# A two-layer transformer on one core: inputs laid out by features, first modulation in quarters

## The chip, the core and the metric

The program runs on one core of a Trainium2 chip. The metric is device time in microseconds (us) of one execution. The engines are PE (TensorE, matrix products), PEld (its weight loads), DVE (VectorE), ACT (ScalarE), POOL (GpSimd) and SP (SyncE, which issues most DMA transfers here). Each engine works its own list of instructions in order, and waits at an instruction for what it needs from other engines.

## The reference, cut to what matters

```python
for l in range(2):                              # DEPTH = 2, D = 1024
    sh1, sc1, gt1, sh2, sc2, gt2 = adaln(c, w_ada[l], b_ada[l])      # silu(c) @ w_ada + b_ada
    csh1, csc1, cgt1, ... = adaln(c_ctx, w_ada[l], b_ada[l])
    h  = rms_norm(x,   g_mix[l]) * (1 + sc1)  + sh1                  # x: 512 x 1024
    hc = rms_norm(ctx, g_mix[l]) * (1 + csc1) + csh1                 # ctx: 256 x 1024
    qa, ka, va, fb, qc, kc, vc = mixer_inputs(h,  w_in[l], q_norm[l], k_norm[l], rope)
    qac, kac, ...              = mixer_inputs(hc, w_in[l], q_norm[l], k_norm[l], None)
    o = concat(global_attention(qa, [kac; ka], ...), fourier_mix(fb), window_attention(qc, ...))
    x = x + gt1 * (o @ w_out[l])
    x = x + gt2 * swiglu(rms_norm(x, g_ffn[l]) * (1 + sc2) + sh2, ...)
    ...                                         # the same for ctx in layer 0
return rms_norm(x, g_final)
```

`mixer_inputs` multiplies by `w_in` and normalises the heads of q and k (root mean square over 64 features, then gains and rotary tables). All is float32.

## The kernel before, in words

Activations lie with features on the 128 partitions, in eight blocks of 128 features (k = 0 to 7), tokens along the free axis: 512 of x, then 256 of the context. A float32 product is made of three products of rounded parts: each operand is split into a high part (`ahi`, `w`, a cast on ACT) and a remainder (`alo`, a subtraction on DVE), and PE adds high x high, high x low and low x high. `split` does this for weights (L103).

The order of the work on each engine comes from the order in which the code issues it, from a scheduler that places instructions by its estimate of times, and from pins: `self.after(i)` and `tc.issue_after(i)` ask that what is issued in them stands behind instruction i. `self.queue` issues DMAs on SP in a line, each behind the last. Buffers come from pools by tag: `tag="hf", bufs=2` gives two buffers, and who asks for a third waits for the readers of one of them. PE's results go to PSUM banks, called `mm`, `fl`, `lg` (the last a pair).

The opening is `first_norm` (L343). Its steps before:

- x comes as four tiles of 128 tokens x 1024 features (`xin`), ACT squares each with a running sum (L360), PE turns the tiles into features (32 transposes, L374) and DVE and ACT copy them (L376, L378).
- The first modulation (the `sh1` and `sc1` columns of `w_ada[0]`, 8 MB) is worked in two halves of its columns (`adaln(0, 0, ..., js=(i, i + 2))`). A half is eight pieces of 512 KB, matmuls with 32 columns (L278), a copy on ACT (L288), four transposes (L296), two additions with the bias on DVE (L301) and the product with the gain (L313, `mod`, writes `smod`).
- `vectors` and `last_gain` load the biases and gains by rows and transpose them.
- Behind each half come its half of `w_in`'s first 512 columns (`qkv_weights(0, half=i)`, 1 MB) and four steps of the norm (`norm_steps`): hf = x * smod * factor on DVE (L461), ahi on ACT (L464), alo on DVE (L466).
- `qkv_first` then makes the products of x, per feature block three products for each of four token tiles (L522 to L524, 96 in all, 128 x 512).
- The context is loaded and transposed the same way (16 transposes), `tables` and `layer_consts` load tables and work out the rotary gains on POOL (`gc`, `gs`, L240 to L244), and `norm_h` normalises the context with 128 x 256 operations. Last, x and the context are written to `xsc` in DRAM, from where the residual is read.

`rstd` makes the factor of a norm: a mean on DVE (L335) and a power on POOL (L339). `bc` broadcasts it with PE (L441).

After the opening `mix` goes on: head norms of the four x tiles (`rms`, squares on ACT L600, sums on DVE L602, power on POOL), rotation and scaling of K on DVE and POOL (`turn_k`, L617 to L623, `kr`), the context's products (48 of 128 x 512, line L90), the value products `va` (L90, 128 x 256), K transposes on PE (L631) and then the scores (L847, L855) with their exponentials on ACT (L859).

Of the kernel before, what the change touches and what calls it, by code (L numbers as in the profile page):

```python
# [46 lines left out]
class Builder:  # L47
# [68 lines left out]
    def raw(self):  # L116
        return self.wp.tile([P, 2048], F32, name=self.nm("raw"), tag="raw", bufs=2)
# [35 lines left out]
    def setup(self):  # L153
        nc, a = self.nc, self.a
        self.ident = self.const([P, P], "ident")
        make_identity(nc, self.ident)
        self.identr = self.const([P, P], "identr", F32R)
        nc.vector.tensor_copy(self.identr, self.ident)
        self.ones = self.const([P, 1], "ones")
        nc.vector.memset(self.ones, 1.0)  # L160
        self.onesr = self.const([P, 1], "onesr", F32R)
        nc.vector.tensor_copy(self.onesr, self.ones)
        self.mhalf = self.const([P, 8], "mhalf")
        nc.vector.memset(self.mhalf, -0.5)
        v2 = self.ip.tile([16, P], F32, name="v2", tag="v2")
        nc.sync.dma_start(v2[0:8], a["c"].rearrange("o (r q) -> (o r) q", q=P))
        nc.sync.dma_start(v2[8:16], a["c_ctx"].rearrange("(r q) -> r q", q=P))
        ps = self.mm()
        nc.tensor.transpose(ps[:, 0:16], v2, self.ident[0:16, 0:16])
        self.ct = self.const([P, KB, 32], "ct")  # L170
        nc.vector.memset(self.ct, 0.0)
        for s in range(2):
            nc.scalar.activation(self.ct[:, :, s], ps[:, 8 * s : 8 * s + 8], AF.Silu)
        vt1 = self.vt1 = self.const([P, P], "vt1")
        self.gfin = self.const([P, KB], "gfin")
        self.bada = [vt1[:, 48 * l : 48 * (l + 1)] for l in range(DEPTH)]
        self.gmix = [vt1[:, 96 + 8 * l : 104 + 8 * l] for l in range(DEPTH)]
        self.gffn = [vt1[:, 112 + 8 * l : 120 + 8 * l] for l in range(DEPTH)]
        self.ada = [self.const([P, 48, 2], f"ada{l}") for l in range(DEPTH)]
        self.smod = [[self.const([P, 8, 2], f"smod{l}{i}") for i in range(2)] for l in range(DEPTH)]  # L180
        self.xsc = self.dp.tile([P, KB, T], F32, name="xsc", tag="xsc")

    def vectors(self):

        nc, a = self.nc, self.a
        v1 = self.ip.tile([P, P], F32, name="v1", tag="v1")
        self.queue(v1[0:96], a["b_ada"].rearrange("l (r q) -> (l r) q", q=P))
        self.queue(v1[96:112], a["g_mix"].rearrange("l (r q) -> (l r) q", q=P))
        self.queue(v1[112:128], a["g_ffn"].rearrange("l (r q) -> (l r) q", q=P))
        ps = self.mm()  # L190
        nc.tensor.transpose(ps[:, 0:128], v1, self.ident)
        nc.vector.tensor_copy(self.vt1, ps[:, 0:128])

    def last_gain(self):
        nc = self.nc
        v = self.ip.tile([KB, P], F32, name="v3", tag="v2")
        self.queue(v, self.a["g_final"].rearrange("(r q) -> r q", q=P))
        ps = self.mm()
        nc.tensor.transpose(ps[:, 0:KB], v, self.ident[0:KB, 0:KB])
        nc.vector.tensor_copy(self.gfin, ps[:, 0:KB])  # L200

    def tables(self, pool):

# [47 lines left out]
    def adaln(self, l, g, raw, psum, tile, hold=KB, js=range(4)):  # L251
# [91 lines left out]
    def first_norm(self):  # L343
        nc, a = self.nc, self.a
        ip = self.fp = self.ip
        xt = [ip.tile([P, T], F32, name=self.nm("xt"), tag=f"xt{k}") for k in range(KB)]
        hi, lo = self.act
        raw = lambda: ip.tile([P, 1024], F32, name=self.nm("ra"), tag="ra", bufs=10)
        halves = [self.adaln(0, 0, raw, f, raw, js=(i, i + 2)) for i, f in enumerate((self.mm, self.fl))]

        def load(src, rng, first):
            r0, r1 = rng
            n = (r1 - r0) // P
            ms = self.small(8, "ims")
            xs = []
            for t in range(n):
                xi = ip.tile([P, D], F32, name=self.nm("xin"), tag="xin", bufs=4)
                self.queue(xi, src[t * P : (t + 1) * P, :])
                sq = ip.tile([P, D], F32, name=self.nm("isq"), tag="isq", bufs=1)
                nc.scalar.activation(sq, xi, AF.Square, accum_out=ms[:, t : t + 1])  # L360
                xs.append(xi)
            for f in first:
                f()
            banks = []
            for k in range(KB):
                if n < TBX:
                    ps = self.mm()
                else:
                    if not banks:
                        lg = self.lg()  # L370
                        banks = [lg[:, 0], lg[:, 1]]
                    ps = banks.pop(0)
                for t in range(n):
                    nc.tensor.transpose(ps[:, t * P : (t + 1) * P], xs[t][:, k * P : (k + 1) * P], self.ident)  # L374
                if k % 2:
                    nc.scalar.copy(xt[k][:, r0:r1], ps[:, 0 : r1 - r0])  # L376
                else:
                    nc.vector.tensor_copy(xt[k][:, r0:r1], ps[:, 0 : r1 - r0])  # L378
            return self.bc(ms[:, 0:n], n)

        bx = load(a["x"][0], XR, halves[0][0:2] + [self.vectors])
        norm = self.norm_steps(hi, lo, xt, bx, XR, 0, 0, 0)
        ws = []
        del halves[0][0:2]
        for i in range(2):
            for f in halves[i]:
                f()
            ws += self.qkv_weights(0, half=i)
            for f in norm[4 * i : 4 * i + 4]:
                f()  # L390
        outs = self.qkv_first(hi, lo, ws)
        bc = load(a["ctx"][0], CR, ())
        self.tables(ip)
        self.last_gain()
        self.line = False
        self.layer_consts(0)
        self.norm_h(hi, lo, xt, bc, CR, 0, 0, 1)
        for k in range(KB):
            nc.sync.dma_start(self.xsc[:, k, :], xt[k])
        return hi, lo, ws, outs  # L400


# [81 lines left out]
    def qkv_weights(self, l, kind=None, half=None):  # L484
        w = self.a["w_in"][l]
        if half is not None:
            return self.load_cols(w[512 * half : 512 * half + 512, 0:512], KB // 2, 512, 2)
        if kind is None:
            return self.qkv_weights(l, half=0) + self.qkv_weights(l, half=1)
        r = self.raw()  # L490
        rv = r.rearrange("p (k w) -> p k w", w=256)
        c = 0
        for c0, n in self.PAIRS[kind]:
            self.nc.sync.dma_start(
                rv[:, :, c : c + n], w[:, c0 : c0 + n].rearrange("(k p) w -> p k w", p=P)
            )
# [573 lines left out]
    def mix(self, l, hi, lo, ws, outs):  # L1070
# [15 lines left out]
        if full:  # L1086
            for tb in (0, 2):
                for f in (rms, turn_k):
                    f(tb)
                    f(tb + 1)  # L1090
            va[0]()
            turn_q(0)
            turn_q(1)
            for f in (rms, turn_k):
# [9 lines left out]
            va[1]()  # L1104
            va[2]()
# [99 lines left out]
    def w_out(self, l, oh, ol):  # L1205
# [639 lines left out]
        pools.close()  # L1845


_INS = [
    "x", "c", "ctx", "c_ctx", "w_ada", "b_ada", "g_mix", "g_ffn", "w_in", "q_norm", "k_norm",
    "sink", "w_out", "w_gate", "w_up", "w_down", "g_final",  # L1850
]
_OUTS = [((1, 512, 1024), "float32")]
_CONSTS = ["cst", "bd", "dcx", "dsx", "dcc", "dsc"]


@with_exitstack
def hybrid_dit_kernel(ctx: ExitStack, tc: tile.TileContext, *args):
    Builder(tc, ctx, dict(zip(_INS + _CONSTS + ["out"], args))).build()


def _constants():
# [64 lines left out]
```

## Time and profile before

| | us |
|---|---|
| median of three runs | 1535.17 (1533.47 to 1535.49) |
| the profiled execution | 1536.4 |
| span of its trace | 1534.6 |
| PE busy in it | 1475.8 (96%) |
| mean granted clock of PE | 0.992 |
| DMA traffic over the span | 211.59 MB, mean 138 GB/s |

All times in the trace start at the span's begin. A row of the timeline gives start, duration, engine, line and operation, then output <- inputs (names without their numbers), the tile's shape, the number of equal instructions, and in brackets how long the engine was idle before and what ended that.

### The profile page before, as it was taken

Reading aid. Unit: us, or ns where it says so; the run is one execution under the profiler, and the core shown is the slowest. Engines: PE = TensorE matmul, PEld = TensorE weight load, DVE = VectorE, ACT = ScalarE, POOL = GpSimd, SP = SyncE. Lnnn points to the kernel's source line nnn. Section 1 sums busy time; section 2 is a strip of 40 time slices with the busy share of each in tenths; the row PEclk is TensorE's granted clock in tenths of the full one; section 3 lists DMA queues with packets and bytes.
Section 4 is the critical chain, followed back from the end, with each engine's and each line's share of the span. In section 5 each row is a group of like instructions: output and inputs, shape, how many; then the busy total and the mean of one; then the engine's idle time right before and its main releaser. Section 6 shows DMA issues by size and latency. Waiting matters only on the chain.

```text
span 1534.6 us, 25580 instructions
## 1 busy us (share of the span) xinstructions
PE 1475.8 (96%) x9769; PEld 1355.9 (88%) x9769; DVE 1127.8 (73%) x1907; ACT 764.1 (50%) x1542; POOL 558.1 (36%) x471
## 2 busy tenths in 40 slices
PE   6999999999999999999999998999999999999997
PEld 3789968688999999999899988987799898988987
DVE  3867577753978778876887875767849877687775
ACT  3556567641754444443435545666637443343434
POOL 0454355310256756552000035353402443443432
PEclk9999999999999999999999999999999999999999
DMA  9510075851043443546893450065441423223311
GB/s 336 194 60 29 1 237 183 290 204 55 29 139 138 151 139 115 172 140 228 295 316 116 142 165 28 28 180 194 159 165 56 133 88 105 89 83 113 108 56 56
DMA packets 124298, 211.59 MB, mean 138 GB/s; under 512 B 6456, under 2 KB 87120, under 8 KB 119056
## 3 DMA queue, kind: packets, MB, share of 16 engines
q1 hardware_dynamic: 116320, 203.92, 39.2%
q0 software_dynamic: 7856, 6.04, 1.9%
q8 instruction: 77, 1.26, 0.3%
q14 instruction: 45, 0.37, 0.1%
HBM read 180.96 MB, written 28.97 MB: 137 GB/s over the span
## 4 chain that ended last, share of the span: by engine, by line
PE 76%; DVE 9%; ACT 4%; issue 4%; DMA 4%; POOL 3%; SPq 0%; POOLq 0%; DVEq 0%; ACTq 0%
PE mm L90 16%; PE lg L90 16%; PE fl L90 13%; DVE w L103 4%; PE mm L1546 4%; PE mm L959 4%; PE lg L1546 4%; PE fl L278 3%; PE mm L951 2%; PE lg L847 2%; ACT w L103 2%; PE lg L855 2%; DMA raw<-in_w_ada_dram 2%; PE fl L1546 1%; PE lg L522 1%
## 5 line engine op out<-in xcount | busy, mean ns | idle before, releaser
L103 DVE TENSOR_TENSOR w<-raw,w 128x512 fp32r<-128x512 f32 (+1 forms) x314 | 285.8, 923 | 95.8 <-ACT w L103 89.3
L103 ACT CAST w<-raw 128x512 fp32r<-128x512 f32 (+1 forms) x314 | 206.9, 676 | 281.3 <-POOL raw L1364 96.7
L90 PE MATMUL fl<-ahi,w 128*128 128x384 f32 (+1 forms) x640 | 154.3, 308 | 0.0
L90 PE MATMUL lg<-ahi,w 128*128 128x384 f32 (+1 forms) x640 | 150.1, 310 | 3.5 <-DVE w L103 2.9
L90 PE MATMUL lg<-th,w 128*128 128x384 f32 (+1 forms) x640 | 149.3, 309 | 2.5 <-ACT u L1385 1.4
L866 POOL TENSOR_TENSOR p<-p,rc 128x768 f32<-128x768 f32 (+2 forms) x84 | 113.3, 1367 | 93.2 <-DVE rc L864 83.7
L90 PE MATMUL mm<-u,w 128*128 128x512 f32 (+1 forms) x576 | 139.5, 377 | 3.4 <-DVE u L103 2.8
L339 POOL TENSOR_TENSOR rs<-ms,mhalf 128x8 f32<-128x8 f32 (+3 forms) x22 | 28.6, 1305 | 289.9 <-DVE ms L335 289.9
L90 PEld LDWEIGHTS lg<-ahi,w 128*128 128x128 f32 x640 | 111.0, 189 | 8.4 <-DVE w L103 4.8
L90 PEld LDWEIGHTS lg<-th,w 128*128 128x128 f32 x640 | 110.6, 189 | 5.2 <-ACT u L1385 2.3
L90 PEld LDWEIGHTS mm<-u,w 128*128 128x128 f32 x576 | 97.1, 189 | 18.7 <-DVE u L103 3.7
L90 PEld LDWEIGHTS fl<-ahi,w 128*128 128x128 f32 x640 | 111.7, 189 | 1.6 <-DVE w L103 0.2
L90 PE MATMUL fl<-w,ahi 128*128 128x256 f32 x544 | 108.0, 291 | 0.6 <-ACT krc L713 0.5
L90 PE MATMUL mm<-ahi,w 128*128 128x256 f32 (+1 forms) x448 | 107.1, 330 | 0.0
L1356 POOL TENSOR_TENSOR s<-raw 128x512 f32<-128x512 f32 x40 | 55.6, 1390 | 136.3 <-DMA raw<-in_w_gate_dram 60.1
L858 DVE TENSOR_REDUCE neg<-lg 128x1 f32<-128x768 f32 (+2 forms) x96 | 81.4, 852 | 26.8 <-PE lg L855 25.8
L103 DVE TENSOR_TENSOR t<-mm,t 128x512 fp32r<-128x512 f32 x108 | 73.9, 686 | 33.7 <-ACT t L103 32.6
L90 PE MATMUL fl<-alo,w 128*128 128x384 f32 (+1 forms) x320 | 98.7, 308 | 0.0
L90 PE MATMUL lg<-tl,w 128*128 128x384 f32 (+1 forms) x320 | 98.7, 308 | 0.0
L90 PE MATMUL lg<-alo,w 128*128 128x384 f32 (+1 forms) x320 | 98.6, 308 | 0.0
L1364 POOL TENSOR_TENSOR raw<-raw 128x512 f32<-128x512 f32 x40 | 62.8, 1569 | 96.1 <-DVE w L103 96.1
L859 ACT ACTIVATE p<-lg,neg 128x768 f32<-128x768 f32 (+2 forms) x84 | 70.3, 837 | 38.7 <-DVE neg L858 30.6
(384 smaller groups left out, 4044.0 us busy)
## 6 DMA issues: line engine op xcount, KB each, us to landing
raw<-in_w_ada_dram SPq DMA_DIRECT2D x40, 1024.0 KB, 4.9
raw<-in_w_gate_dram SPq DMA_DIRECT2D x22, 1024.0 KB, 5.4
raw<-in_w_up_dram SPq DMA_DIRECT2D x22, 1024.0 KB, 5.6
uh<-uh SPq DMA_DIRECT2D x33, 384.0 KB, 4.7
w<-uh SPq DMA_DIRECT2D x33, 384.0 KB, 4.4
wd<-in_w_down_dram SPq DMA_DIRECT2D x47, 256.0 KB, 5.0
raw<-in_w_in_dram SPq DMA_DIRECT2D x11, 1024.0 KB, 5.8
rd<-in_w_down_dram SPq DMA_DIRECT2D x11, 1024.0 KB, 5.0
```

The costliest lines, as they stand in the source:

```text
L90: mm = lambda a, b, **k: self.nc.tensor.matmul(out, a, b, skip_group_check=more, **k)
L103: return self.nc.scalar.copy(hi, src).ins, self.nc.vector.tensor_sub(lo, src, hi).ins
L278: end = nc.tensor.matmul(st["ps"][o : o + 32, :], self.ct[:, k0 + i, :], rs[i][:, j], start=(k0 % hold == 0), stop=((k0 + by) % hold == 0) ...
L847: nc.tensor.matmul(o, qt[:, qs], K1[:, kv, k0 : k0 + w], start=True, stop=False)
L855: nc.tensor.matmul(o, qt[:, qs], K2[:, kv, k0 : k0 + w], start=False, stop=True)
L858: nc.vector.tensor_reduce(ng, lv, axis=AX.X, op=ALU.max, negate=True)
L859: nc.scalar.activation(pt, lv, AF.Exp, bias=ng, accum_out=den[:, i : i + 1])
L866: nc.gpsimd.tensor_tensor(pt, pt, rc[:, i : i + 1].to_broadcast(list(pt.shape)), op=ALU.mult)
L959: nc.tensor.matmul(out[:, r], V[:, kb, kv, :], t[:, c], start=first and n == 0, stop=end and n == len(todo) - 1,)
L1356: nc.gpsimd.tensor_add(s1, a21, a22)
L1364: nc.gpsimd.tensor_sub(a12, a12, a11)
L1546: nc.tensor.matmul(ps, w[:, x, c], u[:, y], start=(not more and k == 0 and j == 0), stop=(k == npc - 1 and j == 2), skip_group_check=True,)
```

## The change

x and the context come as one input `xt`, features on partitions; all vectors as `vec` [128, 152]; the first modulation's weights as `w_first`, cut into four quarters of two feature blocks each. `_laid` arranges them on the host, without arithmetic. In the kernel:

- x is loaded as four DMAs of 512 KB, straight into place (`xin`); the token transposes, their copies and `vectors`, `last_gain` are gone, and so is the first writing of `xsc` (the residual of layer 0 reads `xt` again).
- The statistic of x is made from squares by feature block (ACT and DVE in turn) that PE sums over the partitions (32 matmuls with a column of ones, L384).
- The modulation goes in four quarters: `adaln_part` has four pieces of 512 KB with four 32 x 256 matmuls each (L302), a copy (L313), two transposes (L316), the two additions (L321) and `mod` (L329). Two norm steps and the products of two feature blocks belong to each quarter, and the next quarter's pieces and 256 rows of `w_in` are woven among them.
- The context is loaded as two DMAs into place; its statistic is made by `stat_add` with squares on ACT (L455, L458) in buffers of tag `hf` and additions on POOL (L462); the context's norm follows.

Line numbers shift: products of x L570 to L572, norm L508, L511, L513, `rstd` L351 and L355, `bc` L488, head norms L648 and L650, K transposes L679, scores L895 and L903.

```diff
+    def adaln_part(self, i, raw, psum):
...
+        def step(m):
+            if m == 0:
+                st["ps"] = psum()
+            r = raw()
+            self.queue(r, self.a["w_first"][i, m])
...
+        def last():
+            sb = raw()[:, 0:256]
+            nc.scalar.copy(sb, st["ps"][:, 0:256])
+            pt = st["ps"]
+            for c in range(2):
+                nc.tensor.transpose(pt[:, c * P : (c + 1) * P], sb[:, c * P : (c + 1) * P], self.ident)
...
+            for k in range(2):
+                nc.vector.tensor_tensor(blocks(self.ada[0]), src[:, k], blocks(self.ada[0]) if k else b, op=ALU.add)
+            self.mod(0, 0, slice(2 * i, 2 * i + 2))
...
     def first_norm(self):
...
+        def squares():
...
+                if k % 2:
+                    nc.vector.tensor_tensor(sq, x, x, op=ALU.mult)
+                else:
+                    nc.scalar.square(sq, x)
+                for t in range(TBX):
+                    self.last = nc.tensor.matmul(
+                        ss[:, t : t + 1], sq[:, t * P : (t + 1) * P], self.ones,
...
+        pinned = lambda f: f() if self.last is None else behind(f, self.last)
...
+        first = lambda k, ts=range(TBX): pinned(lambda: self.qkv_first(hi, lo, ws, outs, ts, (k,)))
+        for i in range(3):
+            for f in norm[2 * i : 2 * i + 2]:
                 f()
...
+            mark = self.lowered, self.raised
+            more = parts[i + 1]
+            pinned(more[0])
+            pinned(more[1])
+            first(2 * i)
+            pinned(more[2])
+            ws += behind(lambda: weights(i + 1), *mark)
+            pinned(more[3])
+            more[4]()
+            first(2 * i + 1)
+        load(CR, 4)
+        for k in range(KB):
+            self.stat_add(acc, xt[k], CR, k, nc.gpsimd)
+        for f in norm[6:8]:
+            f()
+        self.normed = self.lowered, self.raised
+        first(6)
+        ss = pinned(lambda: self.stat(acc, CR))
+        first(7, (0, 1))
+        bc = pinned(lambda: self.bc(ss, TBC))
+        first(7, (2, 3))
+        self.normed += (self.last,)
+        with self.after(*self.normed):
+            self.tables(ip)
+            self.line = False
+            self.layer_consts(0)
         self.norm_h(hi, lo, xt, bc, CR, 0, 0, 1)
-        for k in range(KB):
-            nc.sync.dma_start(self.xsc[:, k, :], xt[k])
...
             nc.sync.dma_start(
-                rv[:, :, c : c + n], w[:, c0 : c0 + n].rearrange("(k p) w -> p k w", p=P)
...
+            with self.after(self.dma):
...
-            va[0]()
+            with self.after(*self.normed):
+                va[0]()
```

Three places in the order. POOL, from the opening to the first head norms, before (`rs` is the power of a norm's factor, the first for the context; `gc` and `gs` the rotary gains):

```order
L240 TENSOR_TENSOR gc_530<-cst,g_515 128x256
L241 TENSOR_TENSOR gs_531<-cst,g_515 128x4x32
L244 TENSOR_TENSOR gs_531<-cst,g_515 128x4x32
L240 TENSOR_TENSOR gc_535<-cst,g_515 128x256
L241 TENSOR_TENSOR gs_536<-cst,g_515 128x4x32
L244 TENSOR_TENSOR gs_536<-cst,g_515 128x4x32
L339 TENSOR_TENSOR rs_498<-ms_496,mhalf 128x2
L339 TENSOR_TENSOR rs_658<-ms_656,mhalf 128x8
L620 TENSOR_TENSOR kr_600<-hsq_652 128x128
```

And now (`acc` is the context's sum of squares, `sq` a block's squares):

```order
L462 TENSOR_TENSOR acc<-acc,sq_446 128x256
L462 TENSOR_TENSOR acc<-acc,sq_449 128x256
L217 TENSOR_TENSOR gc_532<-cst,g_517 128x256
L218 TENSOR_TENSOR gs_533<-cst,g_517 128x4x32
L221 TENSOR_TENSOR gs_533<-cst,g_517 128x4x32
L462 TENSOR_TENSOR acc<-acc,sq_452 128x256
L217 TENSOR_TENSOR gc_537<-cst,g_517 128x256
L218 TENSOR_TENSOR gs_538<-cst,g_517 128x4x32
L221 TENSOR_TENSOR gs_538<-cst,g_517 128x4x32
L462 TENSOR_TENSOR acc<-acc,sq_455 128x256
L462 TENSOR_TENSOR acc<-acc,sq_458 128x256
L462 TENSOR_TENSOR acc<-acc,sq_461 128x256
```

The six additions of the context's statistic stand in POOL's row, and the six gain products among them.

DVE at the last two feature blocks of x, before (`hf`, `alo` of 128x512 are x's, those of 128x256 the context's):

```order
L461 SCALAR_TENSOR_TENSOR hf_349<-xt_134,smod_123,mm_225 128x512
L461 SCALAR_TENSOR_TENSOR hf_353<-xt_135,smod_123,mm_225 128x512
L466 SCALAR_TENSOR_TENSOR alo_95<-hf_349,ada_121,ahi_87 128x512
L466 SCALAR_TENSOR_TENSOR alo_96<-hf_353,ada_121,ahi_88 128x512
L461 SCALAR_TENSOR_TENSOR hf_540<-xt_128,smod_123,mm_500 128x256
L461 SCALAR_TENSOR_TENSOR hf_544<-xt_129,smod_123,mm_500 128x256
L466 SCALAR_TENSOR_TENSOR alo_89<-hf_540,ada_121,ahi_81 128x256
L466 SCALAR_TENSOR_TENSOR alo_90<-hf_544,ada_121,ahi_82 128x256
L461 SCALAR_TENSOR_TENSOR hf_548<-xt_130,smod_123,mm_500 128x256
L200 COPY gfin<-mm_512 128x8
```

And now:

```order
L513 SCALAR_TENSOR_TENSOR alo_96<-hf_470,ada_116,ahi_88 128x512
L189 CAST band<-c_513 128x2x128
L190 TENSOR_SCALAR band<-c_513 128x128
L201 TENSOR_SCALAR sinks_522<-ones 128x12
L205 CAST sp_524<-sink_520 128x6
L210 TENSOR_SCALAR nsink_530<-sink_520 128x6
L103 TENSOR_TENSOR w_702<-raw_698,w_701 128x1024
L206 TENSOR_TENSOR sp_525<-sink_520,sp_524 128x6
L207 COPY sinks_522<-sp_524 1x6
L208 CAST sinks_522<-sp_525 1x6
L351 TENSOR_SCALAR ms_497<-mm_486 128x2
L508 SCALAR_TENSOR_TENSOR hf_542<-xin,smod_118,mm_501 128x256
```

Behind the remainder of x's last block now stand the band, the sinks and a weight split (`w`), then the context's mean (`ms`), and only then the first norm of the context; before, that mean (L335) stood seventeen rows ahead of the context's norm.

PE around the end of x's products, before (`lg` x's products, `fl` the value products, `mm_500` the context's factor):

```order
L90 MATMUL fl_772<-w_707,alo_90 128x256
L90 MATMUL fl_772<-w_707,ahi_83 128x256
L90 MATMUL fl_772<-w_708,ahi_83 128x256
L90 MATMUL fl_772<-w_707,alo_91 128x256
L90 MATMUL fl_772<-w_707,ahi_84 128x256
L90 MATMUL fl_772<-w_708,ahi_84 128x256
L90 MATMUL fl_772<-w_707,alo_92 128x256
L441 MATMUL mm_500<-ident,rs_498 128x128 x2
L524 MATMUL lg_357<-w_329,alo_93 128x512
L522 MATMUL lg_357<-w_329,ahi_85 128x512
```

And now:

```order
L570 MATMUL lg_199<-w_412,ahi_88 128x512
L571 MATMUL lg_199<-w_413,ahi_88 128x512
L572 MATMUL lg_199<-w_412,alo_96 128x512
L488 MATMUL mm_501<-ident,rs_499 128x128 x2
L570 MATMUL lg_200<-w_412,ahi_88 128x512
L571 MATMUL lg_200<-w_413,ahi_88 128x512
L572 MATMUL lg_200<-w_412,alo_96 128x512
L570 MATMUL lg_200<-w_412,ahi_88 128x512
L571 MATMUL lg_200<-w_413,ahi_88 128x512
L572 MATMUL lg_200<-w_412,alo_96 128x512
L90 MATMUL fl_766<-w_701,ahi_81 128x256
L90 MATMUL fl_766<-w_702,ahi_81 128x256
```

The value products `fl` stood among x's products of block 4 and now follow those of block 7; the context's factor (L488) stands between the two halves of block 7. Further on, 181 products of 128x256 stood ahead of the first score before, and 221 do now; the K transposes stood behind 13, 35, 72, 74, 120 and 122 of them, and now stand behind 48, 90, 112, 129 and, two of them, 144. These counts include the twelve `fl` products. From the scores on the two lists come together.

More of the change, by code (lines that the diff above doesn't have):

```diff
@@ L164, in setup @@
         nc.vector.memset(self.mhalf, -0.5)
[L165 to L169, printed above, removed]
+        vec = self.const([P, 152], "vec")
+        nc.sync.dma_start(vec, a["vec"])
         self.ct = self.const([P, KB, 32], "ct")
@@ L172, in setup @@
         for s in range(2):
[L173 to L178, printed above, removed]
+            nc.scalar.activation(self.ct[:, :, s], vec[:, 136 + 8 * s : 144 + 8 * s], AF.Silu)
+        self.bada = [vec[:, 48 * l : 48 * (l + 1)] for l in range(DEPTH)]
+        self.gmix = [vec[:, 96 + 8 * l : 104 + 8 * l] for l in range(DEPTH)]
+        self.gffn = [vec[:, 112 + 8 * l : 120 + 8 * l] for l in range(DEPTH)]
+        self.gfin = vec[:, 128:136]
         self.ada = [self.const([P, 48, 2], f"ada{l}") for l in range(DEPTH)]
         self.smod = [[self.const([P, 8, 2], f"smod{l}{i}") for i in range(2)] for l in range(DEPTH)]
[L181 to L200, printed above, removed]
+        self.xsc = self.dp.tile([P, KB, SX], F32, name="xsc", tag="xsc")
     def tables(self, pool):
@@ L345, in first_norm @@
         ip = self.fp = self.ip
-        xt = [ip.tile([P, T], F32, name=self.nm("xt"), tag=f"xt{k}") for k in range(KB)]
+        xt = ip.tile([P, KB, T], F32, name="xin", tag="xin")
         hi, lo = self.act
         raw = lambda: ip.tile([P, 1024], F32, name=self.nm("ra"), tag="ra", bufs=10)
[L349 to L362, printed above, removed]
-                f()
-            banks = []
-            for k in range(KB):
[L366 to L394, printed above, removed]
@@ L395, in first_norm, with load @@
-        self.line = False
-        self.layer_consts(0)
+        parts = [self.adaln_part(i, raw, (self.mm, self.fl)[i % 2]) for i in range(4)]
+        xin = xt
+        def load(rng, step):
+            for k in range(0, KB, step):
+                self.queue(xin[:, k : k + step, rng[0] : rng[1]], a["xt"][:, k : k + step, rng[0] : rng[1]])
+        def squares():
+            ss = self.mm()
+            for k in range(KB):
+                sq = ip.tile([P, SX], F32, name=self.nm("isq"), tag="isq", bufs=4)
+                x = xt[:, k, 0:SX]
+                if k % 2:
[3 more added lines that the diff above has]
+                for t in range(TBX):
+                    self.last = nc.tensor.matmul(
+                        ss[:, t : t + 1], sq[:, t * P : (t + 1) * P], self.ones,
+                        start=(k == 0 and t == 0), stop=(k == KB - 1), skip_group_check=True,
+                    ).ins
+            return ss[:, 0:TBX]
@@ new lines, in first_norm, with behind, weights @@
+        pinned = lambda f: f() if self.last is None else behind(f, self.last)
+        def behind(f, *ins):
+            with self.after(*ins):
+                return f()
+        def weights(i):
+            if i % 2 == 0:
+                self.wraw = self.raw()
+            r = self.wraw[:, 1024 * (i % 2) :]
+            return self.load_cols(a["w_in"][0][256 * i : 256 * i + 256, 0:512], 2, 512, 2, raw=lambda: r)
+        load(XR, 2)
+        ss = squares()
+        pinned(parts[0][0])
+        pinned(parts[0][1])
@@ new lines, in first_norm @@
+        bx = pinned(lambda: self.bc(ss, TBX))
+        xt = [xt[:, k] for k in range(KB)]
+        norm = self.norm_steps(hi, lo, xt, bx, XR, 0, 0, 0)
+        outs = self.qkv_outs()
+        pinned(parts[0][2])
+        ws = behind(lambda: weights(0), self.meant)
+        pinned(parts[0][3])
+        parts[0][4]()
+        acc = ip.tile([P, T], F32, name="acc", tag="acc")
+        first = lambda k, ts=range(TBX): pinned(lambda: self.qkv_first(hi, lo, ws, outs, ts, (k,)))
+        for i in range(3):
+            for f in norm[2 * i : 2 * i + 2]:
+                f()
+            mark = self.lowered, self.raised
[8 more added lines that the diff above has]
+            first(2 * i + 1)
@@ new lines, in first_norm @@
+        load(CR, 4)
+        for k in range(KB):
+            self.stat_add(acc, xt[k], CR, k, nc.gpsimd)
[12 more added lines that the diff above has]
+            self.layer_consts(0)
@@ L1103, in mix @@
             parts.append(self.k_transpose("a", krs, 0, TBX))
-            va[1]()
-            va[2]()
+            with self.after(*self.normed):
+                va[1]()
+                va[2]()
             parts.append(self.k_transpose("a", krs, TBX, TBC))
@@ L1845, in build @@
         pools.close()
[L1848 to L1851, printed above, removed]
+_INS = ["w_ada", "w_in", "q_norm", "k_norm", "sink", "w_out", "w_gate", "w_up", "w_down"]
+_LAID = ["xt", "vec", "w_first"]
 _OUTS = [((1, 512, 1024), "float32")]
@@ L1857, in hybrid_dit_kernel @@
 def hybrid_dit_kernel(ctx: ExitStack, tc: tile.TileContext, *args):
-    Builder(tc, ctx, dict(zip(_INS + _CONSTS + ["out"], args))).build()
+    Builder(tc, ctx, dict(zip(_INS + _LAID + _CONSTS + ["out"], args))).build()
 def _constants():
```

37 lines of the change are left out of this document (32 added, 5 removed).

## The prediction

> **What bounds the kernel now.** I read the shares of busy time first, then PE's waits in the stretch that the change touches, then the same stretch in slices, then the single instructions.
>
> The first line of the page and the waits of PE from 0 to 140 us (us in total, times, longest):
>
> ```profile
> PE 1475.8 (96%) x9769; PEld 1355.9 (88%) x9769; DVE 1127.8 (73%) x1907; ACT 764.1 (50%) x1542; POOL 558.1 (36%) x471
> ...
> PE lg L522 <- ACT ahi L464: 3.9, 2, 3.1
> ...
> PE lg L847 <- ACT p L859: 2.2, 2, 1.9
> ...
> PE mm L278 <- DMA ra<-in_w_ada_dram: 1.2, 1, 1.2
> ```
>
> PE is busy 96% of the time, so whatever delays PE in this opening stretch is paid at the end nearly one for one, as a gain is. Slices of the opening (us; busy time and count on PE, PEld, DVE, ACT, POOL; granted clock, DMA share, GB/s):
>
> ```profile
> 20.00:26.00 6.00, 3.39 (x27) 1.17 (x24) 0.49 (x3) 2.08 (x4) 0.00 (x0) 1.00 1.05 387
> 26.00:28.00 2.00, 0.00 (x0) 0.00 (x0) 1.97 (x5) 2.00 (x5) 0.00 (x0) 0.62 1.05 386
> 30.00:32.00 2.00, 2.00 (x10) 0.20 (x8) 2.00 (x4) 0.10 (x1) 0.00 (x0) 0.50 1.05 385
> 32.00:34.00 2.00, 2.00 (x9) 1.40 (x6) 1.87 (x3) 1.28 (x2) 0.00 (x0) 0.67 1.05 387
> ...
> 99.25:101.16 1.91, 0.03 (x1) 0.00 (x0) 1.91 (x5) 1.85 (x3) 0.00 (x0) 1.00 0.96 399
> ...
> 102.00:104.00 2.00, 2.00 (x12) 2.00 (x11) 1.43 (x3) 1.49 (x3) 0.71 (x2) 0.50 0.01 4
> ```
>
> The DMA engines are full at 387 GB/s; after each of two gaps PE's clock is at half. The instructions between (start, duration; in brackets the idle time before and its releaser):
>
> ```profile
> 22.89 1.06 PE L278 MATMUL mm<-ra,ct 128*32 128x512 f32 x8 [1.23 <-DMA ra<-in_w_ada_dram]
> 24.05 0.59 ACT L288 COPY ra<-mm 128x512 f32<-128x512 f32 x1 [2.70 <-PE mm L278]
> 24.69 0.66 PE L296 MATMUL mm<-ident,ra 128*128 128x128 f32 x4 [0.73 <-ACT ra L288]
> 25.45 0.17 DVE L301 TENSOR_TENSOR ada<-mm,vt 128x16 f32<-128x16 f32 x1 [6.21 <-PE mm L296]
> 26.07 1.41 DVE L461 SCALAR_TENSOR_TENSOR hf<-xt,smod,mm 128x512 f32<-128x512 f32 x2
> 27.66 1.33 ACT L464 ACTIVATE ahi<-hf,ada 128x512 fp32r<-128x512 f32 x2
> 28.43 0.79 PE L522 MATMUL lg<-w,ahi 128*128 128x512 f32 x1 [3.09 <-ACT ahi L464]
> ...
> 62.75 0.89 DVE L466 SCALAR_TENSOR_TENSOR alo<-hf,ada,ahi 128x256 fp32r<-128x256 f32 x2 [0.19 <-ACT ahi L464]
> 62.91 0.39 PE L524 MATMUL lg<-w,alo 128*128 128x512 f32 x1
> 63.59 0.39 PE L524 MATMUL lg<-w,alo 128*128 128x512 f32 x1
> 63.63 1.36 DVE L602 TENSOR_REDUCE hss<-hsq 128x8 f32<-128x512 f32 x2
> 69.20 0.40 POOL L623 TENSOR_TENSOR kr<-kr,rs 128x128 f32<-128x128 f32 x1
> 73.18 1.39 POOL L623 TENSOR_TENSOR kr<-kr,rs 128x128 f32<-128x128 f32 x1
> 78.75 0.76 POOL L623 TENSOR_TENSOR kr<-kr,rs 128x128 f32<-128x128 f32 x2
> 84.16 0.77 POOL L623 TENSOR_TENSOR kr<-kr,rs 128x128 f32<-128x128 f32 x2
> 96.23 0.39 PE L847 MATMUL lg<-K1a,qt 128*128 128x512 f32 x1
> 97.17 0.40 PE L90 MATMUL fl<-w,ahi 128*128 128x256 f32 x2
> 97.87 0.40 PE L90 MATMUL fl<-w,ahi 128*128 128x256 f32 x2
> ```
>
> Read: the last modulation piece lands at 22.8, the chain copy, transposes, sums, norm, rounding takes 5.6, the first product starts at 28.43, x's last ends at 64.0. Three products of 512 columns start in 62.91 to 63.59: 0.229 each. Six of 256 columns lie between 97.17 and 97.87: 0.117 each. The norm of the context ends at 63.64, and in the same moment the head norms begin (L602), from which POOL's scaled K follow at 69.6, 74.6, 79.5 and 84.9: 6.0, 10.9, 15.9 and 21.3 after it.
>
> Groups (count, total, mean ns), the last of the stretch in which the other statistic of this shape is summed on POOL, and the piece of the chain that follows x's products:
>
> ```profile
> L466 DVE SCALAR_TENSOR_TENSOR alo<-hf,ada,ahi 128x256 fp32r<-128x256 f32 x8 | 3.6, 483 | 0.7 <-ACT ahi L464 0.6
> L461 DVE SCALAR_TENSOR_TENSOR hf<-xt,smod,mm 128x256 f32<-128x256 f32 x8 | 3.5, 473 | 0.0
> L103 DVE TENSOR_TENSOR w<-raw,w 128x1024 fp32r<-128x1024 f32 x1 | 1.2, 1214 | 0.0
> ...
> L240 POOL TENSOR_TENSOR gc<-cst,g 128x256 f32<-128x256 f32 x2 | 1.5, 732 | 27.6 <-DMA cst<-in_cst_dram 27.6
> L241 POOL TENSOR_TENSOR gs<-cst,g 128x128 f32<-128x128 f32 x2 | 1.0, 480 | 0.0
> L244 POOL TENSOR_TENSOR gs<-cst,g 128x128 f32<-128x128 f32 x2 | 0.9, 452 | 0.0
> ...
> L415 POOL TENSOR_TENSOR acc<-acc,sq 128x256 f32<-128x256 f32 x10 | 7.4, 735 | 10.4 <-ACT sq L411 10.1
> L339 POOL TENSOR_TENSOR rs<-ms,mhalf 128x2 f32<-128x2 f32 x2 | 1.4, 708 | 1.9 <-DVE ms L335 1.9
> ...
> 63.98 10.88 PE mm L90 x48
> ```
>
> **The change part by part.** I build the new times from these durations; work that is removed (the 48 token transposes, their copies, the vectors' transposes, 3.1 MB written to the scratch copy of x) then drops out by itself. No wait above names that write, so it is worth nothing.
>
> 1. First product. Before, x and half the modulation (6.3 MB) had landed at 22.8; now x, a quarter, its w_in rows and the vectors are 4.8 MB. 1.5 MB at 387 GB/s is 3.9 us: landed at 19.0. From there the old chain, shorter by one norm ahead of the rounding and by half the copy: matmuls 0.3, copy 0.4, transposes 0.5, sums 0.6, norm 0.7, rounding 0.7, handovers 0.3 = 3.5. First product at 22.5: 5.9 earlier.
>
> 2. The quarters' period. The transposes of the next quarter stand in PE's row behind all 24 products of this one. 24 x 0.229 = 5.5, two modulation pieces between them about 0.9 (bounded by 0.5 and 1.1, from eight 512-column matmuls in 1.06), and the chain from L296 at 24.69 to the first rounding (27.66 + 0.67) less a few tenths for the shorter sums, about 3.1: 9.5. In the chain PE has two more pieces, so its idle gap is about 1.7. The data (2.6 MB, 6.8 us) are faster. Block 2 starts at 32.0, block 4 at 41.5; block 5 starts at 45.7 and ends at 48.5, and the last quarter's smod is there at 49.5.
>
> 3. Block 6 waits for POOL. The norm of block 6 (hf, two buffers) takes a buffer that the context's squares hold until POOL's sixth addition, and on ACT its rounding stands behind eight squares. These start when the copy of the last modulation (on ACT, after its last piece just ahead of block 5) is done: about 46.1, first square 46.6, first addition 47.0. POOL's row ahead of hf is six additions, 6 x 0.735 = 4.4, and between them the six gain products, 2 x (0.73 + 0.48 + 0.45) = 3.3; handovers 0.5: 55.2. Unhidden: 5.7. Norm and rounding 1.5: block 6 starts at 56.7, PE idle 7.9. What is queued behind: on DVE the rest of the norm, the band, the sinks and a weight split; on PE everything. The clock will then be at half, as from 28.43 to about 33.3 above: a loss of up to 2.4.
>
> The Trainium skill ("TensorE: Matmul & The Clock Gate", Part 1 on the gate) says that PE drops to half speed after an idle window of about 3.4 us and regains full speed after as long a busy one. By that this gap costs 1.7, and the 1.7-us gaps of the quarters cost nothing. The trace agrees for the long gap (half speed after 3.09 us), but it shows half speed also behind a gap of 1.9 (99.25).
>
> 4. End of x's products: 12 x 0.229 twice, statistics 0.9, the cold loss, and a wait of some tenths, since the context's mean on DVE stands behind band, sinks and a split: 65.6. The 12 value products that stood among x's products before now follow: 67.0, against 64.0 before: +3.0.
>
> 5. The context's norm. It starts when its factor is broadcast, 64.4. Sixteen operations are 8 x 0.473 + 8 x 0.483 = 7.7, two weight splits among them 2.4, a weight cast on ACT ahead of a rounding 1.1: head norms at 75.7, 12.1 later than 63.63. Scaled K at 81.7, 86.6, 91.6, 97.0. PE does 48 context products (10.9) from 67.0, 77.9, then reaches the K transposes behind 36, 78, 100, 117 and 132 narrow products: waits of about 0, 0, 1.5, 0 and 1.4, 2.9 together.
>
> 6. First score. Before: 63.98 + 10.88 + 169 x 0.117 = 94.6, small transposes 1.6, 96.23. After: 67.0 + 10.9 + 209 x 0.117 (24.5) + 1.6 + 2.9 = 106.9: +10.7. Of these 40 x 0.117 = 4.7 are products done ahead of their old place: +6.0.
>
> 7. The cover that these 40 gave. Before they ran among the scores, where PE waited 2.2 for the exponentials. Without them PE may wait up to 4.7 more, or nothing if DVE and ACT keep ahead: I take 1.5, nearer nothing because those engines have less to do there by the same shift.
>
> Sum: +7.5. The residual later reads x from the input and not from the scratch copy, the same bytes. From there the order is the same up to small shifts at the second layer's start, worth nothing. The profiled execution took 1536.4 with a span of 1534.6; the median of the runs is 1535.2, 1.2 lower, and to that I add: 1542.7.
>
> **The rivals.**
>
> A, cold quarters. The three gaps of about 1.7 us lie between the 1.9 (99.25), after which the clock fell, and the 1.23 ahead of 22.89, after which it stayed at 1.00. Each fall costs half of some 3 us, 1.5; three of them 4.5: 1547. For it: the slice at 102. Against: the slice from 20 to 26, and that 1.7 is itself an upper bound if the pieces in the chain land late in it. By the Trainium skill's rule (the page and part named above) only the long gap falls, and A would add nothing.
>
> B, no change. If the squares, by a later or earlier place, do not hold block 6, the 5.7 and some 1.5 of its cold clock go, everything behind moves up by 7 and the K waits stay: 1535.5. For it: POOL idles until its first addition. Against: its row is in order, and the gains stand among the additions.
>
> C, faster. As B, and the head norms come before PE reaches the K transposes. Then 2.9 and the lost cover go as well: 7.5 - 7.2 - 4.4 = -4.1: 1531. It is decided at one place: whether PE stands before the products of block 6 for less than about 1 us, with DVE reaching the head norms before 70. Against: sixteen norms and two splits alone take 10 us behind x's last products.
>
> **How the numbers follow.** My forecast has 0.56, A 0.20, B 0.14, C 0.10. A difference of 0.2%, 3 us, is about what a measurement of this kernel can tell from no change. Forecast and A are slower (0.76 with a little left to B's upper side), B same, C faster. The forecast's own range is 1539 (no cover lost, waits at K half as long) to 1545. The range for 8 in 10 reaches down to 1535.5, B, and up to 1548, A with half of the lost cover.
>
> **What would show it.** Right: first x product near 22.5 (step 1), blocks 9.5 apart (2), an idle PE of 6 to 9 us before block 6 with POOL's sixth addition as releaser and half clock behind it (3), x's products ending near 65.6 (4), the first head norm near 75.7 (5), the first score near 107 (6). Wrong: POOL's additions done before 50, or a head norm of x ahead of the context's norm.

## The result, and the profile after

The changed kernel takes 1548.1 us (median of six runs, 1544.9 to 1554.7) where the kernel before takes 1535.3 in the runs beside it: 1.0086 times as long, 95% interval 1.0062 to 1.0110. That is 12.8 us slower; 7.5 were predicted, and the range ended at 1548.0, 0.1 below the measured time. The profiled execution took 1551.1 with a span of 1549.4.

The waits of PE from 0 to 140 us in the changed kernel (us in total, times, longest):

```profile
PE lg L570 <- ACT ahi L511: 10.9, 4, 7.1
PE mm L384 <- DVE isq L380: 5.8, 1, 5.8
PE fl L90 <- DVE t L770: 1.4, 1, 1.4
PE lg L895 <- ACT p L907: 1.4, 2, 0.8
PE mm L679 <- POOL kr L671: 0.9, 1, 0.9
```

The 7.1 is the one gap ahead of block 6; the three gaps of 1.26 stand ahead of blocks 0, 2 and 4. The instructions of the opening, in order of time:

```profile
5.84 13.81 PE L384 MATMUL mm<-ones,isq 128*128 128x1 f32 x64 [5.84 <-DVE isq L380]
19.59 1.93 PE L302 MATMUL mm<-ra,ct 128*32 128x256 f32 x16
21.45 2.08 PE L488 MATMUL mm<-ident,rs 128*128 128x128 f32 x8
23.45 1.09 PE L302 MATMUL mm<-ra,ct 128*32 128x256 f32 x16
25.04 0.44 PE L316 MATMUL mm<-ident,ra 128*128 128x128 f32 x2 [0.50 <-ACT ra L313]
27.74 0.50 PE L570 MATMUL lg<-w,ahi 128*128 128x512 f32 x1 [1.26 <-ACT ahi L511]
37.57 0.50 PE L570 MATMUL lg<-w,ahi 128*128 128x512 f32 x1 [1.26 <-ACT ahi L511]
47.05 0.50 PE L570 MATMUL lg<-w,ahi 128*128 128x512 f32 x1 [1.26 <-ACT ahi L511]
...
52.30 1.55 POOL L462 TENSOR_TENSOR acc<-acc,sq 128x256 f32<-128x256 f32 x2 [30.94 <-ACT sq L458]
...
57.50 2.32 POOL L462 TENSOR_TENSOR acc<-acc,sq 128x256 f32<-128x256 f32 x3
59.86 0.75 DVE L508 SCALAR_TENSOR_TENSOR hf<-xin,smod,mm 128x512 f32<-128x512 f32 x1 [4.87 <-POOL acc L462]
61.42 0.79 PE L570 MATMUL lg<-w,ahi 128*128 128x512 f32 x1 [7.09 <-ACT ahi L511]
80.88 0.69 DVE L650 TENSOR_REDUCE hss<-hsq 128x8 f32<-128x512 f32 x1 [1.73 <-ACT hsq L648]
...
111.33 0.39 PE L895 MATMUL lg<-K1a,qt 128*128 128x512 f32 x1
```

Against the steps: the first product comes at 27.74, predicted 22.5; blocks 2, 4 at 37.57 and 47.05, so 9.8 and 9.5 apart, predicted 9.5; the norm of block 6 waits for POOL's last addition (59.82) and starts 4.9 behind smod, predicted 5.7; the head norms start at 80.88, predicted 75.7; the first score at 111.33, predicted 107. Everything behind the first product is late by about the 5.2 by which that is late: blocks 2 and 4 by 5.6, block 6 by 4.7, the first score by 4.3.

The clock in the gap (us; PE, PEld, DVE, ACT, POOL; granted clock, DMA share, GB/s):

```profile
56.00:58.00 2.00, 0.00 (x0) 0.00 (x0) 0.00 (x0) 0.42 (x1) 2.00 (x5) 0.92 0.01 4
58.00:60.00 2.00, 0.00 (x0) 0.00 (x0) 0.14 (x1) 0.83 (x2) 1.67 (x3) 0.50 0.00 0
60.00:62.00 2.00, 0.58 (x1) 0.50 (x2) 1.21 (x2) 0.72 (x1) 0.00 (x0) 0.50 0.00 0
62.00:64.00 2.00, 2.00 (x6) 1.60 (x5) 1.17 (x3) 1.04 (x2) 0.00 (x0) 0.50 0.00 0
```

Between the quarters the slices from 28 to 56 us show 1.00, and the clock is back at 0.88 in the slice from 64 to 66.

### The profile page after: what moved, and what is told of

Same layout as the page of the kernel before. It is cut to its first block, busy times and chain, and to the rows that moved or that the text cites. A ratio compares the mean times of both kernels' runs of the same rounds, so it can differ in the third digit from the quotient of the medians.

```text
span 1549.4 us, 25728 instructions
## 1 busy us (share of the span) xinstructions
PE 1485.2 (96%) x9854; PEld 1368.8 (88%) x9854; DVE 1121.7 (72%) x1907; ACT 757.2 (49%) x1535; POOL 555.3 (36%) x477
## 4 chain that ended last, share of the span: by engine, by line
PE 69%; DVE 13%; issue 5%; ACT 5%; POOL 5%; DMA 2%; SPq 0%; POOLq 0%; DVEq 0%; ACTq 0%
PE mm L90 15%; PE lg L90 13%; PE fl L90 12%; DVE w L103 6%; PE mm L1007 4%; PE mm L1596 4%; PE lg L1596 4%; PE mm L999 2%; PE fl L255 2%; PE lg L895 2%; ACT w L103 2%; PE lg L903 1%; PE fl L1596 1%; POOL raw L1414 1%; PE mm L384 1%
## 5 line engine op out<-in xcount | busy, mean ns | idle before, releaser
L355 POOL TENSOR_TENSOR rs<-ms,mhalf 128x8 f32<-128x8 f32 (+3 forms) x22 | 29.0, 1321 | 300.9 <-DVE ms L351 300.9
L90 PEld LDWEIGHTS mm<-u,w 128*128 128x128 f32 x576 | 97.0, 189 | 18.5 <-DVE u L103 2.9
```

The source lines that it names most:

```text
L90: mm = lambda a, b, **k: self.nc.tensor.matmul(out, a, b, skip_group_check=more, **k)
```

## The experiments

**Which cause holds block 6.** Own buffers for the context's squares:

```diff
-            self.stat_add(acc, xt[k], CR, k, nc.gpsimd)
+            self.stat_add(acc, xt[k], CR, k, nc.gpsimd, own=7)
...
-        sq = self.fp.tile([P, SX], F32, name=self.nm("sq"), tag="hf", bufs=2)
+        if own:
+            sq = self.fp.tile([P, r1 - r0], F32, name=self.nm("sq"), tag="csq", bufs=own)
...
```

> The changed kernel, with seven buffers of their own for the context's squares; nothing else. Theory: the norm of block 6 waits for POOL only because the squares hold its two buffers; PE's gap ahead of block 6 falls from 7.1 to the 1.3 of the other quarters, the clock does not fall there, and the time falls by 6 to 7 us, to about 1541.5. Rival: ACT's eight squares ahead of the rounding, or the last modulation itself, are what is late; then the gap stays over 4 us and the time falls by less than 3.

Measured: 1544.9 us (1541.0 to 1549.8), 1.0071 of before (1.0056 to 1.0085). Two waits of PE, and slices:

```profile
57.04 0.50 PE L573 MATMUL lg<-w,ahi 128*128 128x512 f32 x1 [2.26 <-ACT ahi L514]
62.46 0.38 PE L475 MATMUL mm<-ones,acc 128*128 128x1 f32 x2 [0.96 <-POOL acc L465]
...
58.00:60.00 2.00, 2.00 (x7) 1.53 (x6) 2.00 (x6) 0.58 (x1) 1.92 (x4) 0.58 0.00 0
60.00:62.00 2.00, 1.50 (x4) 0.66 (x2) 1.97 (x5) 0.00 (x0) 1.92 (x2) 0.57 0.00 0
```

The gap falls from 7.09 to 2.26: the buffers were what tied the norm to POOL. But the time falls by 3.2 against the changed kernel's median, about half of what was expected. Block 6 starts 4.4 earlier, the end of x's products is only 3.1 earlier (66.8 for 70.0), for two reasons that the expectation lacked. The last quarter has no modulation pieces behind it (two take 1.07 elsewhere) to fill its chain, so its gap is 2.26 and not 1.26, and behind 2.26 the clock did fall (0.58, 0.57). And POOL's additions are still the same chain: the statistic's sums on PE, ahead of block 7, now wait for them (0.96). The hold moved down PE's row by one block.

**The context's statistic earlier.** Own buffers as above, with the load, the squares and their additions ahead of the last quarter, and the sum on PE ahead of block 6:

```diff
+            if i == 2:
+                load(CR, 4)
+                for k in range(KB):
+                    self.stat_add(acc, xt[k], CR, k, nc.gpsimd, own=7)
...
-        load(CR, 4)
-        for k in range(KB):
-            self.stat_add(acc, xt[k], CR, k, nc.gpsimd)
+        ss = pinned(lambda: self.stat(acc, CR))
         for f in norm[6:8]:
             f()
...
-        first(6)
-        ss = pinned(lambda: self.stat(acc, CR))
-        first(7, (0, 1))
+        first(6, (0,))
         bc = pinned(lambda: self.bc(ss, TBC))
-        first(7, (2, 3))
+        first(6, (1, 2, 3))
+        first(7)
```

> The changed kernel, with own buffers for the context's squares, and the context loaded and its statistic made ahead of the last quarter, so that its norm follows x's on DVE at once. Theory: beside the 6 to 7 of the own buffers, the head norms start near the end of x's products (they started at 80.9, 8 us behind it), the K transposes no longer wait, and the time falls by 9 to 10 us, to about 1538.5. Rival: the late head norms cost nothing beyond the 2.3 us of waits in the trace, or the context's data hold up the last quarter: then the time is that of own buffers alone or above it.

Measured: 1541.2 us (1536.9 to 1545.2), 1.0038 (1.0023 to 1.0053). PE ahead of blocks 4 and 6, and the first head norm:

```profile
47.94 0.50 PE L574 MATMUL lg<-w,ahi 128*128 128x512 f32 x1 [1.76 <-ACT ahi L515]
...
58.68 0.80 PE L574 MATMUL lg<-w,ahi 128*128 128x512 f32 x1 [2.26 <-ACT ahi L515]
...
70.11 1.28 DVE L654 TENSOR_REDUCE hss<-hsq 128x8 f32<-128x512 f32 x2 [0.75 <-ACT hsq L652]
```

The head norms come at 70.1, 10.8 earlier than in the changed kernel and 2.5 behind x's last product (67.6), the waits for K are gone, and the time is 6.9 below the changed kernel's median, 3.7 below own buffers alone. Two things in the trace stand against the 9 to 10 expected: the same 2.26 gap with its half clock, as with own buffers, and block 6 itself, which starts 1.6 later than with own buffers alone (58.68 for 57.04), with a gap of 1.76 ahead of block 4. What each of the two costs was not tried. The statement that the late context norm costs something of its own holds; that its data hold up the last quarter does not fit the trace, where no wait of PE from 0 to 140 us ends on a DMA.

**The quarters' chain.** Transposes between the halves of the second block:

```diff
...
             more[4]()                       # now only the copy on ACT
-            first(2 * i + 1)
+            first(2 * i + 1, (0, 1))
+            more[5](True)                   # the transposes, pinned here, sums, smod
+            first(2 * i + 1, (2, 3))
```

> The changed kernel, with the transposes of the next quarter's modulation put between the two halves of the quarter's second block instead of behind it; nothing else. Theory: the chain from the transposes to the next product (2.7 us) stands uncovered in each quarter; six products (1.4 us) now cover a part of it, in two quarters (in the last POOL is later anyway): 2.8 us less, to about 1545.3. Rival: the weights or pieces of the next quarter are what is late; then the period stays 9.5 and the time the same.

Measured: 1546.0 us (1543.3 to 1550.2), 1.0072 (1.0058 to 1.0085): 2.1 below the changed kernel's median, which at this spread can't be told from no change. The profile is clearer: the gaps ahead of blocks 2 and 4 are gone, only these waits for the rounding are left (between them the slice from 30 to 34 us):

```profile
28.80 0.56 PE L579 MATMUL lg<-w,ahi 128*128 128x512 f32 x1 [1.26 <-ACT ahi L520]
...
30.00:34.00 4.00, 4.00 (x22) 2.81 (x25) 1.40 (x3) 0.43 (x1) 0.00 (x0) 0.69 0.89 355
...
61.16 0.80 PE L579 MATMUL lg<-w,ahi 128*128 128x512 f32 x1 [7.08 <-ACT ahi L520]
```

But block 6 starts at 61.16 as before (61.42). In this execution the first product was 1.1 later and the clock fell behind its gap of 1.26 (0.69 from 30 to 34 us), which it did not do in the changed kernel. So of the gain of the chain only some is seen, and what is left of it ends in the same wait of 7.1. What the chain is worth alone stays open.

**The first product.** The squares of x, all made on ACT, are added on DVE, so that PE sums 4 columns and not 32:

```diff
+            nc.scalar.square(sum_, xt[:, 0, 0:SX])
...
-                if k % 2:
-                    nc.vector.tensor_tensor(sq, x, x, op=ALU.mult)
-                else:
-                    nc.scalar.square(sq, x)
-                for t in range(TBX):
-                    self.last = nc.tensor.matmul(ss[:, t : t + 1], sq[:, t * P : (t + 1) * P], self.ones, ...)
+                nc.scalar.square(sq, xt[:, k, 0:SX])
+                nc.vector.tensor_add(sum_, sum_, sq)
+            for t in range(TBX):
+                self.last = nc.tensor.matmul(ss[:, t : t + 1], sum_[:, t * P : (t + 1) * P], self.ones, ...)
```

> The changed kernel, with x's squares (all on ACT) added up over the feature blocks on DVE first, so that PE sums 4 instead of 32 columns. Theory: the 32 float32 sums (64 passes, 5.84 to 19.65 in the trace, 13.8 us) hold back everything by 5.2 us; without them the first product of x comes at about 22.5 instead of 27.7, all that follows moves by 5, and the time falls by about 5 us, to 1543. Rival: the first product is paced by the data or by the broadcast of the factor; it comes at 26 or later and the time falls by less than 1.5 us.

Measured: 1544.7 us (1541.2 to 1548.2), 1.0060 (1.0044 to 1.0076). PE's opening:

```profile
14.74 1.87 PE L383 MATMUL mm<-ones,isum 128*128 128x1 f32 x8 [14.74 <-DVE isum L381]
16.54 1.93 PE L302 MATMUL mm<-ra,ct 128*32 128x256 f32 x16
18.40 2.08 PE L487 MATMUL mm<-ident,rs 128*128 128x128 f32 x8
20.41 1.07 PE L302 MATMUL mm<-ra,ct 128*32 128x256 f32 x16
...
24.68 0.50 PE L569 MATMUL lg<-w,ahi 128*128 128x512 f32 x1 [1.26 <-ACT ahi L510]
```

The first product is 3.06 earlier, not 5, and all that follows moves by the same 3.0 (head norms 77.85 for 80.88). The sums were 3.0 of the 5.2; the broadcast (2.08) stands between the two pairs of pieces and looked like the rest. The time is 3.4 below the changed kernel's median. The broadcast was tried next, behind the pieces:

```diff
-        bx = pinned(lambda: self.bc(ss, TBX))
+        rx = pinned(lambda: self.rstd(ss, TBX, 1.0 / D))
...
         pinned(parts[0][3])
+        pinned(lambda: self.spread(rx, bx, TBX))      # the four broadcasting matmuls
```

> The changed kernel with x's squares added up on DVE first, as in the run that did only this, and with the broadcast of x's factor (2.08 us on PE) moved behind the third and fourth piece of the first quarter's modulation. Theory: of the 5.2 us by which the first product was late, 3.0 were the sums and the other 2.1 this broadcast, which stood ahead of pieces that had landed; the first product now comes at 22.5 to 23.0 (24.7 with the sums alone), and the time falls by another 2 us, to about 1542.5. Rival: the pieces of the first quarter land only then; the first product stays at 24.0 or later.

Measured: 1545.5 us (1541.9 to 1548.0), 1.0057 (1.0036 to 1.0078). The expected gain did not come:

```profile
15.07 1.86 PE L383 MATMUL mm<-ones,isum 128*128 128x1 f32 x8 [15.07 <-DVE isum L381]
16.86 3.64 PE L302 MATMUL mm<-ra,ct 128*32 128x256 f32 x32
20.43 1.89 PE L496 MATMUL mm<-ident,rs 128*128 128x128 f32 x8
...
24.81 0.50 PE L577 MATMUL lg<-w,ahi 128*128 128x512 f32 x1 [1.26 <-ACT ahi L518]
```

PE has work without a gap from 15.07 to 22.5, so the order within it matters little. What matters is that 32 of these matmuls take 3.64 here, while 16 take 1.07 later: PE works at little more than half speed. So the rest of the lateness should be the clock, not the order. The slices can't show this: they print a granted clock of 1.00 here, but the traces hold no clock record for the beginning. The first record, one of full clock, begins at 23.5 us in the changed kernel, 20.5 with the added squares and 22.0 here, and in each it is from about there on that the same work takes its short time. The test is to keep PE busy beforehand with 40 products of zeros, on the same kernel:

```diff
...
+        for i in range(40):
+            self.last = nc.tensor.matmul(zs[:, 0:SX], z[:, 0:P], z, start=True, stop=True).ins
         ss = squares()
```

> The kernel with the added squares and the later broadcast, and ahead of its sums 40 products of zeros (128x512, results unused) that keep PE busy from about 2 us on while it would wait for x. Theory: what is left of the late first product is PE's own work at half speed, since PE idles or does one-column sums up to 16.9: 16 matmuls of the modulation took 1.93 there and 1.07 later. With PE busy before, 32 of them take 2.1 instead of 3.6, and the first product comes at about 23.0 (24.8 without). In the time 1.5 to 2 us less than without, at the edge of what can be told. Rival: the matmuls wait for their data or for POOL's power, and the first product stays at 24.5 or later.

Measured: 1542.4 us (1540.4 to 1543.3), 1.0040 (1.0026 to 1.0053), 3.1 less than without, though the two intervals overlap. The trace is clearer:

```profile
1.60 12.11 PE L407 MATMUL fl<-zeros 128*128 128x512 f32 x40 [1.60 <-DVE zeros L404]
14.61 1.05 PE L383 MATMUL mm<-ones,isum 128*128 128x1 f32 x8 [0.90 <-DVE isum L381]
15.60 1.50 PE L302 MATMUL mm<-ra,ct 128*32 128x256 f32 x24
18.43 0.64 PE L302 MATMUL mm<-ra,ct 128*32 128x256 f32 x8 [1.34 <-DMA ra<-in_w_first_dram]
19.00 1.16 PE L501 MATMUL mm<-ident,rs 128*128 128x128 f32 x8
...
22.64 0.50 PE L582 MATMUL lg<-w,ahi 128*128 128x512 f32 x1 [1.13 <-ACT ahi L523]
```

The first clock record, again of full clock, begins at 7.5 us. The same eight sums take 1.05 for 1.86, the broadcast 1.16 for 1.89, and now PE waits for the data: the last piece of the quarter comes at 18.43. The first product is at 22.64, where the prediction had put it, from data that it had put at 19.0. And with the first product there the time is 1542.4, where the forecast was 1542.7; the kernel before took 1536.7 in the runs beside it, so this one is 5.7 slower, where 7.5 were predicted.

**All together.** Sums, own buffers, early context and the quarters' transposes, without and with the later broadcast, and the latter with the products of zeros:

> All four edits together: squares of x added on DVE first, own buffers for the context's squares, transposes between the halves of each quarter's second block, the context loaded and its statistic made ahead of the last quarter. Theory: the costs lie one behind the other on PE's path and so add up: first product at 24.7 (3.0 earlier), quarters 8.1 apart instead of 9.5 (three times 1.4), no gap over 2 us ahead of block 6 (5 and the half clock, 7 together), head norms at the end of x's products: about 17 us less than the changed kernel, 1531, and 4 below the kernel before. Rival: the data set the pace once the chain is shorter (2.6 MB a quarter, 6.8 us, and the context's 1 MB ahead of the last): the quarters stay 9 apart and the time is no lower than 1536.

> The four edits together and the broadcast of x's factor behind the first quarter's pieces. Theory: 2 us less than the four alone, 1529; first product at 22.5 to 23.0. Rival: the quarters are paced by the data from here on, so that the earlier first product is lost again at the second or third quarter, and the time is that of the four edits.

> The kernel with all five edits (median 1530), and the same 40 products of zeros. Theory: first product at about 22.5 instead of 23.9, 1 to 2 us less in the time. Rival: as with the later broadcast, which brought x's products forward by 3 us in the profile and the time by nothing measurable: what is gained ahead of the first score is lost behind it, where the exponentials set the pace; the time stays within 1 us of 1530.

Measured: 1529.6 us (0.9967, 0.9952 to 0.9981), 1530.1 (0.9957, 0.9939 to 0.9974) and 1527.2 (0.9941, 0.9927 to 0.9956): all three below the kernel before, the last by 9.5 us (1536.7 in the runs beside it). With the four edits the blocks 0, 2, 4 and 6 start at 25.55, 35.37, 43.76 and 52.45: the wait ahead of block 6 is down to 0.34, and the last two quarters take 8.4 and 8.7, near the 8.1 expected. Not as expected, the head norms start at 65.3, still 6.3 behind the end of x's products (59.0). The later broadcast alone gave nothing that can be told, the time that its rival gave, but not for the rival's reason: the gain isn't lost at the quarters, for the quarters take 8.1, 8.4 and 8.7, and the first score comes at 94.3 in this profile and at 97.6 in that of the four edits, where the clock fell behind the first product (0.50 from 26 to 28 us, behind a gap of 1.26). Where those 3.4 us go behind the first score was not looked into. The products of zeros gave 2.9 on top; their first product came at 22.7 for 23.9, 1.1 earlier, so the mechanism accounts for 1.1 of it, and the rest lies within the runs' spread. Waits of PE from 0 to 140 us in the last:

```profile
PE lg L595 <- ACT ahi L536: 1.6, 2, 1.1
PE fl L413 <- DVE zeros L410: 1.6, 1, 1.6
PE mm L389 <- DVE isum L387: 1.3, 1, 1.3
PE mm L302 <- DMA ra<-in_w_first_dram: 1.3, 1, 1.3
PE lg L920 <- ACT p L932: 1.1, 2, 0.8
PE mm L1032 <- DVE t L103: 0.8, 2, 0.5
...
93.48 0.39 PE L920 MATMUL lg<-K1a,qt 128*128 128x512 f32 x1
```

The first score stands at 93.5, 2.7 ahead of the kernel before (96.2), with 38 more narrow products (128x256) done by then (4.4 us): 7.1 ahead in all.

## Why the prediction was right or wrong

- **Step 1 failed: the first product.** It took the data as the only thing to wait for and charged PE 0.3 us of matmuls. It left out PE's own work ahead of the transposes: 32 sums (64 passes, 13.8 us), the broadcast (2.1) and the pieces (3.0), nearly all of it at about half speed. Removing most sums moved the product by 3.0; a PE kept busy beforehand then moved it by another 2.2 to 22.6, and the time to 1542.4 (1540.4 to 1543.3), where the forecast was 1542.7. This one term is 5.2 us, and the total was short by 5.3. That the two agree so closely is partly luck: at the gate (below) the profiled kernel is 11.4 behind, 3.9 more than was predicted, and the rest comes from a later stretch that the prediction had put at nothing.
- Step 2 held: 9.8 and 9.5 for 9.5. The gap of PE in it was 1.26 and not 1.7, since two pieces took 1.07.
- Step 3 held in its mechanism, from the buffers to POOL's row, and in its size: 4.9 between smod and the norm, predicted 5.7; idle 7.1, predicted 7.9; and half clock behind it, as foreseen. What the runs added is that without the buffers the same chain of POOL is met again at the statistic.
- Steps 4 and 5 held, shifted by the 5.2: end of x's products 4.4 later than predicted, head norms 5.2. The waits for K and the wait on the same chain (0.9 and 1.4) are 2.3, predicted 2.9.
- Step 6 held, shifted in the same way: the first score is 15.1 later than before, predicted 10.7. Step 7 came near in its size, but its reason isn't shown. By the first product of the first layer's gate, 387.7 before and 399.1 now, 11.4 are left, so 3.7 were given back; the prediction had 4.7 less 1.5, 3.2. The 1.5 were to be longer waits of PE for the exponentials, and these did not grow: from the first score to the gate they are 3.7 now and were 4.2 before. What took the missing 1.0 is open. Behind that this profiled execution lost 3.4 more (a wait of 3.7 for L1437 among them); that stretch has the same instructions in both kernels, and it wasn't tried what brings this.
- Rival A didn't come true: three gaps of 1.26, no fall of the clock. A gap near 1.7 was met only later, 1.76 ahead of block 4 with the early context, and the slices behind it show 1.00. But with the quarters' transposes and with the four edits together the clock fell behind a gap of 1.26, so the length of its gaps alone doesn't explain why no quarter of the changed kernel went cold. B and C fell with the wait for POOL.
- The rule of the Trainium skill on the gate ("TensorE: Matmul & The Clock Gate", Part 1: idle for about 3.4 us to fall) agrees with the 7.1 gap and the 1.26 gaps of the changed kernel; the 2.26 gap of own buffers, with 0.58 behind it, goes against its letter, as do the 1.26 gap with the quarters' transposes (0.69 behind it) and the 1.9 gap of the kernel before (the 3.09 gap there, which the prediction took for agreement, is also a little short of 3.4).

## What to carry to other kernels

Count what the new path puts on PE itself, not only when its data land: a sum over partitions by one-column products took two passes for each 128 tokens of a feature block here, each with a 128x128 weight, at 0.22 us a pass in this opening (0.13 with PE kept busy before). Before tying a statistic to a slower engine, look whose buffers it borrows: a shared tag of two put a chain of 7.5 us on POOL (52.30 to 59.82) between two blocks of the main product, and own buffers only moved the meeting point until the statistic itself came earlier. Edits along one chain don't add up when taken singly: alone, the added squares gave 3.4 us, the quarters' transposes 2.1 and the early context with its own buffers 6.9, 12.4 in all, with runs that spread over 7 to 8 us each; together they gave 18.5.

## What was not expected of the hardware

- Work of one column didn't bring PE's clock up. After 13.8 us of sums without a gap, 16 matmuls still took 1.93 us, and 1.09 only a little later, where the trace's first record of full clock begins (23.5 us); after 12 us of 512-column products, with that record at 7.5 us, the same sums took 0.13 each instead of 0.22 to 0.23. The granted clock reads 1.00 from 0 to 20 us in the slices of both, because there is no record that says otherwise, so in an opening the durations have to be read, not that column. The slice of the changed kernel:

```profile
0.00:20.00 20.00, 14.16 (x68) 13.93 (x72) 3.67 (x12) 5.26 (x9) 2.60 (x10) 1.00 0.91 298
```

- The length of a gap doesn't tell alone whether the clock falls. It fell behind 2.26 us, and in two runs behind 1.26; it stayed at 1.00 behind the changed kernel's three gaps of 1.26 and behind one of 1.76. In every trace the clock records change only at moments a multiple of 3.41 us apart (in the changed kernel at 23.54, 57.67 and 64.50 us). With the quarters' transposes the gaps of 0.49 and 1.26 ahead of the first product lie in one such stretch, 25.69 to 29.10, with PE busy for 0.51 of it; in the changed kernel the same two gaps lie in two stretches, busy for 0.71 and 0.76. So where a gap lies may count as much as its length; no run was made to test this.
